# Values of the differential attention by two token tiles with 512 columns instead of two heads with 256, and the second of their products ahead of diff_in(2)

## The chip, the cores and the metric

The kernel runs on one core of a Trainium2 chip, as one launch. The metric is device time in microseconds: the median of 3 runs of the kernel before is 1768.67 us (1768.25 to 1769.67). One execution was profiled; its span is 1766.6 us.

## The reference

A trunk of two layers works on 512 tokens of 1024 features. Each layer norms its input, projects it with one matrix w_in, and mixes it in three branches: differential attention with four heads, a convolution module, and a neighbourhood attention ("natten"). Sigmoid gates merge them, then follow a SwiGLU FFN and a gated input embedding. What matters here, cut:

```python
q, k = apply_rope(q, cos, sin), apply_rope(k, cos, sin)   # per head 2 x 64 columns
v = va.reshape(B, S, HA, DV_A).transpose(0, 2, 1, 3)      # 4 heads x 128 columns
s = jnp.einsum('bhcqd,bhckd->bhcqk', qi, k) * scale
a = jax.nn.softmax(s, axis=-1)
a = a[:, :, 0] - lam * a[:, :, 1]
o = jnp.einsum('bhqk,bhkd->bhqd', a, v)
```

`va` is the normed input (512 x 1024) times 512 columns of w_in.

## The kernel before, in words

All products run as three fp32r matmuls: every operand is split into a high part (ACT copies it, L147) and a low part (DVE subtracts, L161), and high x high, high x low and low x high are added in PSUM. `split` does both. `weights()` brings one weight tile of up to 128 x 1024 (512 KB): a DMA into `wr` on SP's queue, the high part `wh` by ACT, the low part `wl` by DVE. Each of the three has 3 buffers, so a transfer waits until the low part of the tile three earlier is done. These three steps get a priority 400 ahead of their place; the order of ACT, DVE, POOL and of the queues follows from priorities, a scheduler decides it when the program is built. The order of PE is the order in which the code is written. PSUM has 3 buffers `mm`, 2 `sc` (scores), 2 `tr` (transposes) and 1 `av`.

A layer calls in turn glu, natten_in and natten_v, then `diff_in(0)`, `diff_v(0)`, `diff_in(1)`, `gate_c(0)`, `diff_in(2)`, `diff_v(1)`, `diff_in(3)`, the other gates, and after them the branch products, merges, w_o, the FFN and the embedding. `diff_in(head)` projects queries and keys of one head. For both, ACT copies the product to `rp`, four DMAs on SP's queue write the rotated copy (L846), DVE multiplies both with the rope tables and adds them ("rope rows"), splits the sum into `kh` and `rp`, and DMAs stack the parts in `qk` and `x`. Then it queues four attention units with `later(unit, delay, gap)`. Time for these is counted in ticks of four chunks, a chunk being three matmuls of a projection: a unit starts `delay` ticks after it was queued. A unit makes scores (4 matmuls, `diff_sc`), their maximum (TENSOR_REDUCE on DVE), the exponentials on ACT, a reciprocal and a factor with lambda, and `diff_a` on DVE; every second unit then transposes two `diff_a` (`diff_tr`), splits them to `pt`, and multiplies with the values (`diff_av`). The natten units run the same way, their products being `natten_mm` (3 buffers `mm` are shared with the projections), evicted in two DVE rows `natten_y`.

`diff_v(g)` calls `values()`: for a pair of heads g, the 256 columns of the pair for all 512 tokens, the tokens stationary and the weights streaming (L619, L621, L623). Two accumulators hold two token tiles each; 8 k-tiles x 4 token tiles x 3 matmuls make 96 matmuls of 256 columns. The weights of a pair are two tiles of 512 KB. Eight evictions of 128x256 to `v` follow in a layer (ACT and DVE each). The taps of the convolution (`conv_z`, L164, 240 in all) are put behind single operations as background work of DVE: one behind the first rope row of each projection, for instance. `gate_b` takes its buffers from `v`.

Of the kernel before, what the change touches and what calls it, by code (L numbers as in the profile page):

```python
# [20 lines left out]
P = 128  # L21
L = 2
# [4 lines left out]
KD = 8  # L27
# [38 lines left out]
class Net:  # L66
# [365 lines left out]
    def layer(self, i, h, xsrc, xs):  # L432
        self.i, self.h = i, h
        zs, cs = [], []
        self.todo = self.taps(zs, cs)
        self.glu(zs)
        if i == 0:
            self.lambdas()
        yc, ya, yb = [], [], []
        sn, sd = {}, {}  # L440
        self.natten_in(0, sn, yc)
        self.drain(self.renorm)
        self.h = self.hs
        self.natten_v(sn)
        last = self.glu_last(zs)
        self.natten_in(1, sn, yc)
        next(last)
        self.natten_in(2, sn, yc)
        next(last)
        self.natten_in(3, sn, yc)  # L450
        acc, gb = [], []
        self.diff_in(0, sd, ya)
        self.diff_v(0, sd)
        self.diff_in(1, sd, ya)
        self.gate_c(acc, 0)
        self.diff_in(2, sd, ya)
        self.diff_v(1, sd)
        self.diff_in(3, sd, ya)
        for m in range(1, KD):
            self.gate_c(acc, m)  # L460
        for m in range(2):
            self.gate_b(gb, m, AF.Copy, None)
        for g in acc + gb:
            self.act(g, g, AF.Sigmoid, table="sigmoid")
        self.branch_c(acc, yc)
        for m in range(2, 4):
            self.gate_b(gb, m, AF.Sigmoid, "sigmoid")
# [12 lines left out]
        h = self.ffn(h, x)  # L480
        return self.ple(h, x, xs, self.inputs())
# [118 lines left out]

        yield from self.norm(st[0], CB, (3, 1), done)

    def values(self, ap, parts):


        mm = self.nc.tensor.matmul
        accs = [self.ps("mm", (P, 2, 256)) for _ in range(2)]
        for o in range(0, KD, 4):
            wh, wl = self.weights(ap[:, o * 256:(o + 4) * 256], 1024)
            both = [(k, t) for k in range(o, o + 4) for t in range(4)]  # L610
            if o == 0:

                both.sort(key=lambda kt: kt[1] // 2)
            for n, (k, t) in enumerate(both):
                s = slice((k - o) * 256, (k - o + 1) * 256)
                out = accs[t // 2][:, t % 2, :]
                ts = slice(t * P, (t + 1) * P)

                mm(out, self.h[k][:, 0, ts], wh[:, s], start=k == 0 and t % 2 == 0,  # L619
                   stop=False, skip_group_check=True)  # L620
                mm(out, self.h[k][:, 0, ts], wl[:, s], start=False, stop=False,  # L621
                   skip_group_check=True)
                mm(out, self.h[k][:, 1, ts], wh[:, s], start=False,  # L623
                   stop=k == KD - 1 and t % 2 == 1, skip_group_check=True)
                if n % 2:
                    self.chunk()
        vs = []
        for acc in accs:
            v = self.sb("v", [P, 2, 512], F32R)
            for t in range(2):  # L630
                for hi, lo, a in parts(v[:, t], acc[:, t]):
                    self.split(hi, lo, a)
            vs.append(v)
        return vs

# [168 lines left out]
    def gate_b(self, gs, m, func, table):  # L804
        self.phase = "gateb"
        ps = self.proj(OFF_G + D + m * P)
        if m % 2 == 0:
            gs += self.parts_of("v", [512], 2)
        self.background(self.act(gs[m], ps, func, table=table), self.bg["gateb"])

# [19 lines left out]
    def diff_in(self, head, st, ys):  # L830
# [21 lines left out]
            self.stack(nat, low, st4[:, 2 * s:2 * s + 2], k2 if s else None)  # L852
        box = dict(s0=self.sb("sm", [P, 4]))
        for qt in range(4):
            self.later(self.diff_unit(head, qt, st4, k2, st, box, ys), 6 if head else 7, 2)

    def diff_v(self, g, st):
        self.phase = "diff"
        st["v", g] = self.values(self.a["w_va"][self.i, g], lambda v, a: ((v[:, 0:256], v[:, 256:512], a),))

    def diff_unit(self, head, qt, st4, k2, st, box, ys):

# [513 lines left out]
    return np.ascontiguousarray(w).reshape(*lead, m // P, P, (k // P) * P)  # L1376


def _vblocks(w):
    w = w.reshape(L, KD, P, 2, 256).transpose(0, 3, 2, 1, 4)  # L1380
    return np.ascontiguousarray(w).reshape(L, 2, P, KD * 256)
# [52 lines left out]
def _layout(v):  # L1434
# [4 lines left out]
    for i in range(L):  # L1439
# [17 lines left out]
        "w_va": _vblocks(w_in[:, :, OFF_VA:OFF_VA + 512]),  # L1457
# [26 lines left out]
```

## Time and profile before

| what | number |
|---|---|
| median of 3 runs | 1768.67 us (1768.25 to 1769.67) |
| span of the profiled execution | 1766.6 us |
| PE busy, share of the span | 1759.3 us, 100% |
| DVE busy | 1408.6 us, 80% |
| ACT busy | 885.5 us, 50% |
| chain that ended last | PE 92%, DVE 4%, DMA 2%, ACT 2% |
| matmuls of the values | 384 of 256 columns |

The profile shows one execution. Matmuls are pipelined, so a row's duration on PE overlaps the next row; what a matmul costs is read from the start of one to the start of the next. Rows of DVE and ACT overlap by some 0.1 us in the same way. A row of the timeline has its start, its duration, engine, line, operation and tiles, and in brackets the idle time before it and what ended that.

### The profile page before, as it was taken

How to read it: one execution, taken by the hardware profiler on the slowest of the kernel's cores; microseconds unless marked ns; L12 is line 12 of the kernel's file. 1: busy time of each engine (PE TensorE's matmuls, PEld its weight loads, DVE VectorE, ACT ScalarE, POOL GpSimd, SP SyncE). 2: the span in 40 equal slices, each digit the busy share in tenths (PEclk: the TensorE clock that was granted, in tenths of full speed). 3: DMA queues.
4: the chain of work that ended last, by engine and by line, in shares of the span. 5: the costliest groups of instructions: out<-in, count | busy, mean ns of one | idle time of the engine just before them, and what ended most of it. 6: DMA issues, size and time to landing. Idle time of an engine off the chain costs nothing.

```text
span 1766.6 us, 27127 instructions
## 1 busy us (share of the span) xinstructions
PE 1759.3 (100%) x10146; PEld 1551.8 (88%) x10146; DVE 1408.6 (80%) x2354; ACT 885.5 (50%) x1529; POOL 98.4 (6%) x114
## 2 busy tenths in 40 slices
PE   9999999999999999999999999999999999999998
PEld 7888888888899899998888888888888998989987
DVE  7967988998898587787777688889887976867776
ACT  5576555325565254454545655552356643534444
POOL 0000000000111010100000000000001110101000
PEclk9999999999999999999999999999999999999999
DMA  6575641334757365544446655322356674655332
GB/s 231 158 186 160 162 123 54 102 100 150 222 153 196 106 173 156 137 126 127 151 137 173 180 148 154 108 73 94 101 183 194 168 179 118 172 141 156 99 104 96
DMA packets 112548, 253.95 MB, mean 144 GB/s; under 512 B 14368, under 2 KB 23328, under 8 KB 112416
## 3 DMA queue, kind: packets, MB, share of 16 engines
q1 hardware_dynamic: 99024, 227.83, 42.0%
q0 software_dynamic: 12672, 23.07, 8.1%
q8 instruction: 80, 1.31, 0.3%
q10 hardware_dynamic: 720, 1.31, 0.2%
q14 instruction: 52, 0.43, 0.1%
HBM read 214.41 MB, written 7.34 MB: 126 GB/s over the span
## 4 chain that ended last, share of the span: by engine, by line
PE 92%; DVE 4%; DMA 2%; ACT 2%; issue 1%; SPq 0%; POOL 0%; ACTq 0%; POOLq 0%; DVEq 0%
PE ffn_mm L1034 4%; PE ffn_mm L1036 4%; PE ffn_mm L182 4%; PE ffn_mm L181 4%; PE ffn_mm L183 4%; PE ffn_mm L1035 4%; PE ffn_sc L1036 3%; PE ffn_sc L1034 3%; PE ffn_sc L1035 3%; PE mergea_mm L182 2%; PE mergea_mm L183 2%; PE mergea_mm L181 2%; PE gateb_mm L182 2%; PE gateb_mm L183 2%; PE gateb_mm L181 2%; PE wo_mm L182 2%
## 5 line engine op out<-in xcount | busy, mean ns | idle before, releaser
L164 DVE SCALAR_TENSOR_TENSOR conv_z<-glu_z,pre_par,conv_z 128x512 f32<-128x512 f32 x240 | 179.6, 748 | 3.5
L147 ACT ACTIVATE ffn_wh<-ffn_wr 128x1024 fp32r<-128x1024 f32 (+1 forms) x92 | 92.8, 1015 | 111.9 <-PE ffn_mm L182 81.4
L1004 POOL DMA_DIRECT2D ffn_qk<-w_fu x88 | 78.1, 978 | 605.6 <-DMA ffn_qk<-w_fu 289.7
L161 DVE TENSOR_TENSOR ffn_wl<-ffn_wr,ffn_wh 128x1024 fp32r<-128x1024 f32 (+1 forms) x92 | 107.4, 1173 | 5.3 <-ACT ffn_wh L147 4.6
L161 DVE TENSOR_TENSOR ffn_t<-ffn_mm,wo_rb 128x512 f32<-128x512 f32 (+1 forms) x64 | 38.7, 605 | 68.4 <-PE ffn_mm L183 68.4
L147 ACT ACTIVATE mergea_wh<-mergea_wr 128x1024 fp32r<-128x1024 f32 (+1 forms) x32 | 27.1, 848 | 96.8 <-PE mergea_mm L182 79.5
L147 ACT ACTIVATE ffn_wh<-ffn_qk 128x1024 fp32r<-128x1024 f32 x44 | 46.7, 1061 | 37.1 <-PE ffn_mm L182 15.9
L161 DVE TENSOR_TENSOR ffn_wl<-ffn_qk,ffn_wh 128x1024 fp32r<-128x1024 f32 x44 | 53.9, 1224 | 10.7 <-ACT ffn_wh L147 10.7
L161 DVE TENSOR_TENSOR ffn_t<-ffn_t,ffn_t 128x512 f32<-128x512 f32 (+1 forms) x46 | 31.3, 680 | 31.9 <-ACT ffn_t L147 31.4
L147 ACT ACTIVATE natten_e<-natten_e,natten_s 128x192 f32<-128x192 f32 (+1 forms) x88 | 39.3, 474 | 25.2 <-DVE natten_s L726 21.9
L181 PE MATMUL ffn_mm<-ffn_v,ffn_wh 128*128 128x512 f32 x132 | 51.4, 389 | 0.0
L182 PE MATMUL ffn_mm<-ffn_v,ffn_wh 128*128 128x512 f32 x132 | 51.4, 389 | 0.0
L183 PE MATMUL ffn_mm<-ffn_v,ffn_wl 128*128 128x512 f32 x132 | 51.3, 389 | 0.0
L181 PE MATMUL ffn_mm<-ffn_y,ffn_wh 128*128 128x512 f32 x132 | 51.3, 389 | 0.0
L182 PE MATMUL ffn_mm<-ffn_y,ffn_wh 128*128 128x512 f32 x132 | 51.3, 389 | 0.0
L183 PE MATMUL ffn_mm<-ffn_y,ffn_wl 128*128 128x512 f32 x132 | 51.3, 389 | 0.0
L147 ACT ACTIVATE diff_a<-diff_sc,diff_s 128x512 f32<-128x512 f32 x32 | 22.0, 687 | 57.1 <-DVE diff_s L919 57.0
L1036 PE MATMUL ffn_mm<-wo_h,ffn_wl 128*128 128x256 f32 x176 | 49.8, 283 | 0.0
L1036 PE MATMUL ffn_sc<-wo_h,ffn_wl 128*128 128x256 f32 x176 | 49.8, 283 | 0.0
L1035 PE MATMUL ffn_sc<-wo_h,ffn_wh 128*128 128x256 f32 x176 | 49.8, 283 | 0.0
L1035 PE MATMUL ffn_mm<-wo_h,ffn_wh 128*128 128x256 f32 x176 | 49.8, 283 | 0.0
L1034 PE MATMUL ffn_sc<-wo_h,ffn_wh 128*128 128x256 f32 x176 | 49.8, 283 | 0.0
(879 smaller groups left out, 6539.8 us busy)
## 6 DMA issues: line engine op xcount, KB each, us to landing
ffn_qk<-w_fu POOLq DMA_DIRECT2D x88, 256.0 KB, 5.7
ffn_wr<-w_fg SPq DMA_DIRECT2D x44, 512.0 KB, 3.7
ffn_wr<-w_fd SPq DMA_DIRECT2D x32, 448.0 KB, 4.1
ffn_r<-w_fu SPq DMA_DIRECT2D x44, 256.0 KB, 4.2
ffn_qk<-w_fg SPq DMA_DIRECT2D x44, 256.0 KB, 4.0
ffn_qk<-w_fu SPq DMA_DIRECT2D x44, 256.0 KB, 4.2
natten_wr<-w_in SPq DMA_DIRECT2D x16, 512.0 KB, 4.3
diff_wr<-w_in SPq DMA_DIRECT2D x16, 512.0 KB, 4.2
```

What stands on the lines that cost most here:

```text
L147: i = self.nc.scalar.activation(out, in_, func, **kw)
L161: return self.nc.vector.tensor_tensor(out, a, b, op)
L164: return self.nc.vector.scalar_tensor_tensor(out, a, s, b, op0, op1)
L181: mm(out, wh, ah, start=first, stop=False)
L182: mm(out, wh, al, start=False, stop=False)
L183: mm(out, wl, ah, start=False, stop=last)
L1004: nc.gpsimd.dma_start(q, wu[:, lo], accum_op=ALU.add)
L1034: mm(out, wh[:, c], bh, start=first and k == 0, stop=False, skip_group_check=True)
L1035: mm(out, wh[:, c], bl, start=False, stop=False, skip_group_check=True)
L1036: mm(out, wl[:, c], bh, start=False, stop=k == 3, skip_group_check=True)
```

## The change

`values(ap, half)` now makes one half of the tokens (two tiles of 128) for all 512 columns: two accumulators of 128 x 512, one for each token tile, 8 k-tiles x 2 token tiles x 3 matmuls, 48 matmuls of 512 columns. `diff_v(0)` makes tokens 0 to 255, `diff_v(1)` tokens 256 to 511, each with the whole of w_va, whose layout on the host becomes k-tile by k-tile with 512 columns; each call loads it as four tiles of 512 KB. Every unit now needs both halves, so `diff_v(1)` moves ahead of `diff_in(2)`, and the first head's units start 9 ticks after they are queued instead of 7. A half is evicted in two splits of 128x512. Two of the gates' buffers come from `kh`, since `v` is held in another shape.

```diff
         self.gate_c(acc, 0)
+        self.diff_v(1, sd)
         self.diff_in(2, sd, ya)
-        self.diff_v(1, sd)
...
-    def values(self, ap, parts):
+    def values(self, ap, half):
...
-        accs = [self.ps("mm", (P, 2, 256)) for _ in range(2)]
-        for o in range(0, KD, 4):
-            wh, wl = self.weights(ap[:, o * 256:(o + 4) * 256], 1024)
-            both = [(k, t) for k in range(o, o + 4) for t in range(4)]
...
-                mm(out, self.h[k][:, 0, ts], wh[:, s], start=k == 0 and t % 2 == 0,
-                   stop=False, skip_group_check=True)
...
+        accs = [self.ps("mm") for _ in range(2)]
+        for o in range(0, KD, 2):
+            wh, wl = self.weights(ap[:, o * 512:(o + 2) * 512], 1024)
+            for k in (o, o + 1):
+                s = slice((k - o) * 512, (k - o + 1) * 512)
+                for t, out in enumerate(accs):
+                    hi, lo = (a[:, (2 * half + t) * P:(2 * half + t + 1) * P] for a in self.halves(self.h[k]))
+                    mm(out, hi, wh[:, s], start=k == 0, stop=False)
+                    mm(out, hi, wl[:, s], start=False, stop=False)
+                    mm(out, lo, wh[:, s], start=False, stop=k == KD - 1)
                     self.chunk()
...
-            for t in range(2):
-                for hi, lo, a in parts(v[:, t], acc[:, t]):
-                    self.split(hi, lo, a)
+            self.split(v[:, 0], v[:, 1], acc)
...
-        if m % 2 == 0:
+        if m == 0:
+            gs += [self.sb("kh", [P, 512]) for _ in range(2)]
+        elif m % 2 == 0:
             gs += self.parts_of("v", [512], 2)
...
-            self.later(self.diff_unit(head, qt, st4, k2, st, box, ys), 6 if head else 7, 2)
+            self.later(self.diff_unit(head, qt, st4, k2, st, box, ys), 6 if head else 9, 2)
...
-        cs = slice((head % 2) * P, (head % 2) * P + P)
+        cs = slice(head * P, head * P + P)
...
-                v = st["v", head // 2][kp][:, u].rearrange("p (a b) -> p a b", a=2)
+                v = st["v", kp][u]
```

On PE the second product of values stands behind the gate. In layer 0, these are PE's rows at the end of `gate_c(0)` before (L181 to L183 are the projections' matmuls, `diff_mm` an accumulator in an `mm` buffer):

```order
849 L181 MATMUL gatec_mm_1861<-glu_h_558,gatec_wh_1863 128x512
850 L182 MATMUL gatec_mm_1861<-glu_h_558,gatec_wh_1863 128x512
851 L183 MATMUL gatec_mm_1861<-glu_h_558,gatec_wl_1864 128x512
852 L181 MATMUL diff_mm_1926<-glu_h_386,diff_wh_1928 128x512
853 L182 MATMUL diff_mm_1926<-glu_h_386,diff_wh_1928 128x512
854 L183 MATMUL diff_mm_1926<-glu_h_386,diff_wl_1929 128x512
```

And at the same place of the changed kernel:

```order
797 L181 MATMUL gatec_mm_1805<-glu_h_558,gatec_wh_1807 128x512
798 L182 MATMUL gatec_mm_1805<-glu_h_558,gatec_wh_1807 128x512
799 L183 MATMUL gatec_mm_1805<-glu_h_558,gatec_wl_1808 128x512
800 L614 MATMUL diff_mm_1868<-diff_wh_1871,glu_h_386 128x512
801 L615 MATMUL diff_mm_1868<-diff_wl_1872,glu_h_386 128x512
802 L616 MATMUL diff_mm_1868<-diff_wh_1871,glu_h_386 128x512
803 L614 MATMUL diff_mm_1869<-diff_wh_1871,glu_h_386 128x512
```

Where the queries of head 2 followed, the values now follow, and they take two `mm` buffers at once (1868 and 1869), four rows after the gate's last.

DVE's rows in the same stretch of layer 0, from the rope rows of head 1's queries (`diff_rp`) on, before (`diff_wl` are low parts of weights, `diff_v` an eviction of values, `diff_s` with `diff_sc` a maximum of scores):

```order
262 L161 TENSOR_TENSOR diff_rp_1742<-diff_rp_1742,diff_r_1315 128x512
263 L164 SCALAR_TENSOR_TENSOR conv_z_370<-glu_z_321,pre_par_67,conv_z_370 128x512
264 L161 TENSOR_TENSOR diff_wl_2010<-diff_wr_2008,diff_wh_2009 128x1024
265 L161 TENSOR_TENSOR diff_rp_1743<-diff_rp_1743,diff_r_1317 128x512
266 L924 RECIPROCAL diff_s_1810<-diff_s_1810 128x1
267 L161 TENSOR_TENSOR diff_rp_1742<-diff_rp_1742,diff_rp_1743 128x512
268 L161 TENSOR_TENSOR diff_v_1685<-diff_mm_1503,diff_v_1685 128x256
```

And of the changed kernel, from the same rope row to the first low part of weights behind the natten eviction:

```order
261 L161 TENSOR_TENSOR diff_rp_1702<-diff_rp_1702,diff_r_1315 128x512
262 L161 TENSOR_TENSOR diff_wl_1906<-diff_wr_1904,diff_wh_1905 128x1024
263 L164 SCALAR_TENSOR_TENSOR conv_z_370<-glu_z_321,pre_par_67,conv_z_370 128x512
264 L161 TENSOR_TENSOR diff_rp_1703<-diff_rp_1703,diff_r_1317 128x512
265 L161 TENSOR_TENSOR diff_rp_1702<-diff_rp_1702,diff_rp_1703 128x512
266 L161 TENSOR_TENSOR diff_v_1647<-diff_mm_1503,diff_v_1647 128x512
267 L161 TENSOR_TENSOR natten_y_1314<-natten_mm_1824,natten_y_1314 64x512
268 L161 TENSOR_TENSOR diff_rp_1702<-diff_rp_1702,diff_kh_1713 128x512
269 L161 TENSOR_TENSOR natten_y_1314<-natten_y_1314,natten_mm_1824 64x512
270 L910 TENSOR_REDUCE diff_s_1836<-diff_sc_1837 128x1
271 L910 TENSOR_REDUCE diff_s_1836<-diff_sc_1843 128x1
272 L161 TENSOR_TENSOR diff_wl_1924<-diff_wr_1922,diff_wh_1923 128x1024
```

The two `natten_y` rows stand earlier in the changed order, the reciprocal and the maximum rows of head 0 later, and the low parts are of `w_va` (further ones, 1958 and 2001, 2079, stand in rows 277, 282 and 287; the second `diff_a` is row 289).

On SP's queue, the weight transfers between the key transfers of head 0 and the rotated copies of head 1 (L846), before:

```order
97 L175 DMA diff_wr_2008<-w_in 128x1024
98 L664 DMA diff_qk_1319<-diff_kh_1490 64x512 x2
99 L664 DMA diff_x_1320<-diff_kh_1490 64x512 x2
100 L664 DMA diff_qk_1319<-diff_rp_1479 64x512 x2
101 L664 DMA diff_x_1320<-diff_rp_1479 64x512 x2
102 L175 DMA diff_wr_2093<-w_va 128x1024
103 L846 DMA diff_rp_1743<-diff_rp_1742 32x512
104 L175 DMA diff_wr_2179<-w_va 128x1024
105 L846 DMA diff_rp_1743<-diff_rp_1742 32x512 x3
```

And in the changed kernel (the copies are at L837 there):

```order
99 L175 DMA diff_wr_1870<-w_va 128x1024
100 L653 DMA diff_qk_1319<-diff_rp_1399 64x512
101 L653 DMA diff_qk_1319<-diff_kh_1490 64x512 x2
102 L175 DMA diff_wr_1904<-w_va 128x1024
103 L653 DMA diff_x_1320<-diff_kh_1490 64x512
104 L175 DMA diff_wr_1922<-w_va 128x1024
105 L653 DMA diff_x_1320<-diff_kh_1490 64x512
106 L653 DMA diff_qk_1319<-diff_rp_1479 64x512 x2
107 L653 DMA diff_x_1320<-diff_rp_1479 64x512 x2
108 L837 DMA diff_rp_1703<-diff_rp_1702 32x512
109 L175 DMA diff_wr_1956<-w_va 128x1024
110 L837 DMA diff_rp_1703<-diff_rp_1702 32x512 x3
```

The two tiles 1904 and 1922 now stand among the key transfers, where 2093 stood behind them; behind the first copy one weight tile stands in both.

More of the change, by code (lines that the diff above doesn't have):

```diff
@@ L601, in conv @@
         yield from self.norm(st[0], CB, (3, 1), done)
-    def values(self, ap, parts):
+    def values(self, ap, half):
         mm = self.nc.tensor.matmul
-        accs = [self.ps("mm", (P, 2, 256)) for _ in range(2)]
-        for o in range(0, KD, 4):
-            wh, wl = self.weights(ap[:, o * 256:(o + 4) * 256], 1024)
-            both = [(k, t) for k in range(o, o + 4) for t in range(4)]
[L611 to L619, printed above, removed]
-                   stop=False, skip_group_check=True)
[L621 to L625, printed above, removed]
+        accs = [self.ps("mm") for _ in range(2)]
[8 more added lines that the diff above has]
+                    mm(out, lo, wh[:, s], start=False, stop=k == KD - 1)
                     self.chunk()
@@ L854, in diff_in @@
         for qt in range(4):
-            self.later(self.diff_unit(head, qt, st4, k2, st, box, ys), 6 if head else 7, 2)
+            self.later(self.diff_unit(head, qt, st4, k2, st, box, ys), 6 if head else 9, 2)
     def diff_v(self, g, st):
         self.phase = "diff"
-        st["v", g] = self.values(self.a["w_va"][self.i, g], lambda v, a: ((v[:, 0:256], v[:, 256:512], a),))
+        st["v", g] = self.values(self.a["w_va"][self.i], g)
     def diff_unit(self, head, qt, st4, k2, st, box, ys):
@@ L1376, in _blocks @@
     return np.ascontiguousarray(w).reshape(*lead, m // P, P, (k // P) * P)
-def _vblocks(w):
-    w = w.reshape(L, KD, P, 2, 256).transpose(0, 3, 2, 1, 4)
-    return np.ascontiguousarray(w).reshape(L, 2, P, KD * 256)
 def _wide(w):
@@ L1456, in _layout @@
         "w_in": _blocks(w_in),
-        "w_va": _vblocks(w_in[:, :, OFF_VA:OFF_VA + 512]),
+        "w_va": _wide(w_in[:, :, OFF_VA:OFF_VA + 512]),
         "w_vc": _wide(w_in[:, :, OFF_VC:OFF_VC + 512]),
```

## Prediction

> **What bounds the kernel now.** I read the page first, from its top: the busy times, the granted clock and the chain that ended last.
>
> ```profile
> span 1766.6 us, 27127 instructions
> PE 1759.3 (100%) x10146; PEld 1551.8 (88%) x10146; DVE 1408.6 (80%) x2354; ACT 885.5 (50%) x1529; POOL 98.4 (6%) x114
> PEclk9999999999999999999999999999999999999999
> PE 92%; DVE 4%; DMA 2%; ACT 2%; issue 1%; SPq 0%; POOL 0%; ACTq 0%; POOLq 0%; DVEq 0%
> ```
>
> TensorE is the bound: busy for the whole span, at its full granted clock in all 40 slices, and 92% of the chain. So the time is the sum of the distances from the start of one matmul to the start of the next, plus the few places where PE waits. VectorE holds only 4% of the chain, but it is the second engine, and its 80% is a mean. The table by stage says more about the stretch in which the change works:
>
> ```profile
> 170.00:180.00 10.00, 8.92 (x17) 1.00 0.48 138
> 180.00:190.00 10.00, 9.84 (x18) 1.00 0.40 109
> 1056.00:1066.00 10.00, 9.87 (x18) 1.00 0.41 105
> ```
>
> The columns are the stretch, its length, busy time of DVE, granted clock, DMA share and GB/s. In layer 0 VectorE has 0.16 us to spare between 180 and 190, in layer 1 0.13 us between 1056 and 1066. Both are in or next to the place to which the second product of values is moved. There anything that VectorE gets on top must show up as time.
>
> **The change part by part.** *The matmuls.* Before, a stretch of 48 matmuls of 256 columns begins at the first row below and ends where the next group starts; the other two rows give the distance of 512-column matmuls.
>
> ```profile
> L619 PE MATMUL diff_mm<-diff_wh,glu_h x64: 277/283/364, 142.6 to 208.3; 128*128 128x256 f32 x64
> 150.28 0.30 PE L619 MATMUL diff_mm<-diff_wh,glu_h 128*128 128x256 f32 x1
> 156.06 0.25 PE L722 MATMUL natten_sc<-natten_qk 128*128 128x192 f32 x1
> ...
> 139.55 0.39 PE L181 MATMUL diff_mm<-glu_h,diff_wh 128*128 128x512 f32 x1
> 140.23 0.39 PE L181 MATMUL diff_mm<-glu_h,diff_wh 128*128 128x512 f32 x1
> ```
>
> 48 matmuls take 156.06 - 150.28 = 5.78 us, 0.1204 each; three of 512 columns take 140.23 - 139.55 = 0.68, 0.2267 each, and 24 of them 5.44. (The duration column, 283 ns, holds the modelled end of a pipelined matmul and is not the cost.) A stretch thus saves 0.34 us. L619 has 64 rows in layer 0, three lines like it make 192, both layers 384: eight stretches, **-2.7 us**. That is all the change can gain on PE's own work. [...]
>
> *The weights.* Both halves need all of w_va, so it is loaded and split twice: 8 tiles of 512 KB in each layer for 4, which adds 4 transfers on SP's queue, 4 high parts on ACT, 4 low parts on DVE. ACT's 50% hides its four of 1.05 us. The low parts are no free work, by the DVE rows around the place (layer 0):
>
> ```profile
> 167.05 1.23 DVE L161 TENSOR_TENSOR diff_wl<-diff_wr,diff_wh 128x1024 fp32r<-128x1024 f32 x1 [0.53 <-ACT diff_wh L147]
> ...
> 173.27 0.69 DVE L161 TENSOR_TENSOR diff_rp<-diff_rp,diff_r 128x512 f32<-128x512 f32 x1 [0.99 <-DMA diff_rp<-diff_rp]
> 173.88 0.75 DVE L164 SCALAR_TENSOR_TENSOR conv_z<-glu_z,pre_par,conv_z 128x512 f32<-128x512 f32 x1
> 174.54 1.22 DVE L161 TENSOR_TENSOR diff_wl<-diff_wr,diff_wh 128x1024 fp32r<-128x1024 f32 x1
> 175.68 0.69 DVE L161 TENSOR_TENSOR diff_rp<-diff_rp,diff_r 128x512 f32<-128x512 f32 x1
> ...
> 177.01 0.42 DVE L161 TENSOR_TENSOR diff_v<-diff_mm,diff_v 128x256 fp32r<-128x256 f32 x1
> 177.34 0.21 DVE L164 SCALAR_TENSOR_TENSOR diff_s<-diff_s,glu_nlam,diff_sm 128x1 f32<-128x1 f32 x1
> ...
> 179.78 0.69 DVE L161 TENSOR_TENSOR natten_y<-natten_mm,natten_y 64x512 fp32r<-64x512 f32 x1
> 180.51 0.69 DVE L919 TENSOR_REDUCE diff_s<-diff_sc 128x1 f32<-128x512 f32 x1
> ...
> 183.09 0.16 DVE L924 RECIPROCAL diff_s<-diff_s 128x1 f32<-128x1 f32 x1
> ...
> 183.53 0.75 DVE L164 SCALAR_TENSOR_TENSOR diff_a<-diff_e,diff_s,diff_a 128x512 f32<-128x512 f32 x1
> 184.20 1.28 DVE L919 TENSOR_REDUCE diff_s<-diff_sc 128x1 f32<-128x512 f32 x2
> 185.40 0.68 DVE L161 TENSOR_TENSOR diff_rp<-diff_rp,diff_r 128x512 f32<-128x512 f32 x1
> ```
>
> From start to start: a low part of weights 1.14 (174.54 to 175.68), a rope row of 128x512 0.61, a conv tap 0.66, natten_y 0.73, a reduce 0.60 (two from 184.20 to 185.40), reciprocal and lambda row 0.44 (183.09 to 183.53), diff_a 0.67, an eviction of v with 256 columns 0.33. One of 512 columns stands nowhere in the trace; I take 0.61, like the rope row, whose two operands have the same shape; its ends are 0.33 (as 256 columns) and 0.66 (twice that). Four low parts (4.56) less the eviction (8 x 0.33 to 4 x 0.61, -0.2) add 4.4 us of DVE work to each layer.
>
> *The order.* By the order rows above, the second stretch of values now follows gate_c(0) directly. PE reaches it early. Before, the gate's last matmul ends where diff_in(2) begins:
>
> ```profile
> 174.18 0.39 PE L183 MATMUL gatec_mm<-glu_h,gatec_wl 128*128 128x512 f32 x1
> 174.66 0.98 PE L763 MATMUL natten_mm<-natten_pt,natten_v 128*128 128x256 f32 x6
> ...
> 179.36 0.39 PE L181 MATMUL diff_mm<-glu_h,diff_wh 128*128 128x512 f32 x1
> 185.71 1.03 PE L876 MATMUL diff_tr<-pre_ident,diff_a 128*128 128x128 f32 x8
> 189.35 0.39 PE L828 MATMUL diff_sc<-diff_qk 128*128 128x512 f32 x1
> 190.26 0.39 PE L181 MATMUL diff_mm<-glu_h,diff_wh 128*128 128x512 f32 x1
> ```
>
> From 179.36 I take off two stretches (0.68), the first score group of head 0, which its longer delay moves behind (0.91, 189.35 to 190.26), and the 0.25 by which natten_mm was late (174.18 to 174.66 is 0.48, one matmul 0.23; it waited for ACT's copy of the raw key projection, which now runs before it). PE would start the second stretch at 177.5. 48 matmuls (10.88) and two score groups (1.82) later, at 190.2, it wants the transposes of diff_a.
>
> VectorE's side starts from the rope row at 173.27, which waited 0.99 us for the rotated copies on SP's queue:
>
> ```profile
> 168.30 0.39 SPq L175 DMA_DIRECT2D diff_wr<-w_va  x1
> 168.74 6.40 SPq L846 DMA_DIRECT2D diff_rp<-diff_rp  x4
> ```
>
> The copies stand behind the weight transfer at 168.30, which needs the buffer that the low part of 167.05 frees at 168.28. In the changed order one such tile, also of w_va, stands there too. PE's 0.7 us lead would draw all this forward, the two low parts more between 140 and 168 push it back; I leave it at 173.27. From there DVE has, by its order up to the second diff_a, 5 low parts (5.70), 8 rope rows (4.88), one v eviction (0.61), 2 natten_y (1.46), 2 taps (1.32), 5 reduces (3.00), 2 pairs of reciprocal and lambda (0.88) and 2 diff_a (1.34): 29 rows, 19.2 us without a gap, until 192.5. Against 190.2 PE waits 2.3 us. Most of it shows earlier: the second accumulator of the stretch needs the PSUM slot of natten_mm, freed by the second natten_y, the ninth row, at 173.27 + 6.3 = 179.6, while PE wants it at 178.2 (three matmuls after 177.5): 1.4 us, and about 0.9 more at the transposes. Before, diff_a was done at 184.20 and its transposes came at 185.71; the stretch had 1.5 us in hand.
>
> Layer 1 the same way:
>
> ```profile
> 1048.63 0.69 DVE L161 TENSOR_TENSOR diff_rp<-diff_rp,diff_r 128x512 f32<-128x512 f32 x1 [1.86 <-DMA diff_rp<-diff_rp]
> 1048.74 0.39 PE L183 MATMUL gatec_mm<-ple_h,gatec_wl 128*128 128x512 f32 x1
> 1049.14 0.97 PE L763 MATMUL natten_mm<-natten_pt,natten_v 128*128 128x256 f32 x6
> 1056.98 0.39 PE L828 MATMUL diff_sc<-diff_x,diff_qk 128*128 128x512 f32 x1
> 1057.76 0.40 PE L828 MATMUL diff_sc<-diff_x,diff_qk 128*128 128x512 f32 x1
> 1060.73 1.03 PE L876 MATMUL diff_tr<-pre_ident,diff_a 128*128 128x128 f32 x8
> ```
>
> Its stalls that go are 0.17 at natten_mm (0.40 for 0.23) and 0.32 at the scores (1056.98 to 1057.76 is 0.78 for two matmuls), 0.5 in all. It lies 1060.73 - 185.71 = 875.0 later, less the 0.25 by which more of its stalls go than in layer 0: PE is ready at 1065.0; DVE is done at 1048.63 + 19.2 = 1067.8. PE waits 2.8.
>
> *What costs nothing.* The other 48 matmuls of each layer come between 143 and 156, where the new low parts have the idle time ahead of 167 and PE needs no VectorE result at once. The kh buffers for two gates and the larger v tiles come free well before their next user. If that cover is gone, the price is at most the two low parts there, 2.3 us in each layer.
>
> *Sum,* against the profiled execution: -2.7 - 0.25 - 0.5 + 2.3 + 2.8 = +1.65, 1768.3 by its span. The median, 1768.67, lies 2.1 above that span, so I add 2.1: **1770.3 us**. About 0.2% (3.5 us) is what a measurement of this kernel can tell from no change.
>
> **The rivals.** *VectorE keeps up.* If the rope row starts 2.3 to 2.8 us sooner, no new wait appears and the gain stays: -2.7 - 0.75, 1765.2. For it speaks the idle time ahead of the rope rows, 0.99 and 1.86 us; against it that they waited for DMAs which the change does not bring forward by more than 0.7 us.
>
> *The queue (slower).* Three w_va tiles now stand on SP's queue ahead of the copies, among the key transfers of head 0, where two weight tiles stood. Each moves 512 KB, on a DMA share that is 0.48 already. If the rotated copies land later, the run of 29 rows starts later, and with no slack in it PE waits for all of that, twice: it decides from about 1 us a layer (1772.3). Half of such a transfer's 4.2 us landing, 2.1 a layer, gives 1774.5.
>
> ```profile
> diff_wr<-w_in SPq DMA_DIRECT2D x16, 512.0 KB, 4.2
> ```
>
> *The matmuls gain nothing.* In the quoted 512 rows the weights are stationary; here the tokens are, and the weights stream. If these cost 0.241 a piece like a pair of 256, -2.7 is gone: 1773.0. Against it: both kinds load 128 columns of weights, and the 256-column rows stream weights already.
>
> **How the numbers follow.** Forecast 0.53, VectorE keeps up 0.17, the queue 0.23, no gain 0.04, the rest for what I have not seen. The forecast's own range is 1768.9 (rope rows 0.7 sooner, twice) to 1771.8 (v eviction and pairs dearer). The range goes from 1765.2, VectorE keeping up, to 1774.5, the queue. Faster by over 0.2% (under 1765.1) needs the second case and something more: 0.06. Slower (over 1772.2): the queue, no gain and the forecast's upper tail, 0.30. Within: 0.64.
>
> **What would show it.** In the changed profile: 192 matmuls of values at 0.227 from start to start; a pause of 1 to 2 us ahead of the fourth matmul of the second stretch, released by DVE natten_y, and one ahead of diff_tr, released by DVE diff_a; DVE without idle time for 19 us after a rope row near 173. I am wrong if the rope row starts before 171, if the pause names a DMA, or if a new wait stands outside these stretches.

## The result and the profile after

The changed kernel takes 1779.72 us (median, 1779.11 to 1780.21), the kernel before 1769.43 beside it: ratio 1.006, 95% interval 1.0048 to 1.0072. It is 10.3 us slower; 1770.3 was forecast, and the range ended at 1774.5. The profiled execution has a span of 1777.3 us against 1766.6, so the 10.7 us can be looked for in its trace.

The first lines of the page after, to be laid beside those of before:

```profile
span 1777.3 us, 26765 instructions
PE 1760.8 (99%) x9954; PEld 1544.1 (87%) x9954; DVE 1413.5 (80%) x2354; ACT 893.4 (50%) x1529; POOL 97.4 (5%) x114
PE 90%; DVE 5%; ACT 1%; DMA 1%; issue 1%; SPq 0%; POOL 0%; ACTq 0%; DVEq 0%; POOLq 0%
```

DVE is busy for 4.9 us longer: its eight further low parts take 9.7 us, the larger evictions 1.2 less than the smaller ones did, and its other rows are a little shorter in this execution. PE's share of the chain fell by two points: PE waits. The stages outside the attention's stretch, from the branch merges to the FFN and the embedding, last the same to 0.01 us in both traces. All the time is between the first diff_in and the last attention unit, and 0.96 us at the very start, where the 512-column matmuls are 0.427 us apart until 4.9 us before and until 7.2 us after, then 0.23 (PE's first glu row starts at 26.77 and 27.73).

PE's rows with idle time ahead of them, in that stretch of the changed kernel, layer 0 and then layer 1 (in brackets the idle time and what ended it; what the pause adds from start to start is about 0.16 more):

```profile
150.43 0.41 PE L752 MATMUL natten_mm<-natten_a,natten_x 128*128 128x128 f32 x2 [0.50 <-ACT diff_wh L147]
180.71 0.47 PE L614 MATMUL diff_mm<-diff_wh,glu_h 128*128 128x512 f32 x1 [0.74 <-DVE natten_y L161]
193.57 0.98 PE L867 MATMUL diff_tr<-pre_ident,diff_a 128*128 128x128 f32 x7 [0.48 <-DVE diff_a L164]
230.95 0.62 PE L231 MATMUL diff_tr<-pre_ident,diff_rc 128*128 128x128 f32 x4 [3.02 <-DVE diff_pt L161]
...
1029.59 0.41 PE L752 MATMUL natten_mm<-natten_a,natten_x 128*128 128x128 f32 x2 [0.50 <-ACT diff_wh L147]
1059.49 0.47 PE L614 MATMUL diff_mm<-diff_wh,ple_h 128*128 128x512 f32 x1 [0.41 <-DVE natten_y L161]
1072.36 0.98 PE L867 MATMUL diff_tr<-pre_ident,diff_a 128*128 128x128 f32 x7 [0.46 <-DVE diff_a L164]
1109.71 1.08 PE L231 MATMUL diff_tr<-pre_ident,diff_rc 128*128 128x128 f32 x4 [3.02 <-DVE diff_pt L161]
```

The second and third row of each layer are the two pauses that the prediction named, at the places and with the releasers that it named. The first and the fourth it did not have. The fourth is the largest by far: the second transposes of the norm that closes head 0 (L231 spreads the row `diff_rc` over all partitions) need one of the two `tr` buffers in PSUM, and that one still holds the transposed probabilities of head 1, until DVE has split them (`diff_pt`). What DVE did meanwhile:

```profile
220.65 0.69 DVE L220 TENSOR_REDUCE diff_sm<-diff_tr 128x4 f32<-128x512 f32 x1 [1.42 <-PE diff_tr L217]
...
222.53 0.69 DVE L161 TENSOR_TENSOR diff_rp<-diff_rp,diff_r 128x512 f32<-128x512 f32 x1
223.14 0.54 DVE L549 TENSOR_SCALAR conv_z<-glu_z,pre_par 128x512 f32<-128x512 f32 x1
223.60 0.68 DVE L161 TENSOR_TENSOR diff_rp<-diff_rp,diff_r 128x512 f32<-128x512 f32 x1
...
224.32 0.69 DVE L161 TENSOR_TENSOR diff_rp<-diff_rp,diff_rp 128x512 f32<-128x512 f32 x1
...
226.39 0.68 DVE L161 TENSOR_TENSOR diff_rp<-diff_rp,diff_kh 128x512 fp32r<-128x512 f32 x1
226.99 0.68 DVE L161 TENSOR_TENSOR diff_rp<-diff_rp,diff_r 128x512 f32<-128x512 f32 x1
...
228.26 0.68 DVE L161 TENSOR_TENSOR diff_rp<-diff_rp,diff_r 128x512 f32<-128x512 f32 x1
228.86 0.74 DVE L164 SCALAR_TENSOR_TENSOR diff_a<-diff_e,diff_s,diff_a 128x512 f32<-128x512 f32 x1
229.52 0.68 DVE L161 TENSOR_TENSOR diff_rp<-diff_rp,diff_rp 128x512 f32<-128x512 f32 x1
230.12 1.28 DVE L161 TENSOR_TENSOR diff_pt<-diff_tr,diff_pt 128x512 fp32r<-128x512 f32 x2
```

DVE was idle for 1.42 us before 220.65 and then worked almost without a gap to 230.12. Seven rope rows (by their sequence, four of head 2's keys and three of head 3's queries), two taps and a weight split stand ahead of diff_pt in its order; ACT's half of the same split had run at 225.12. The kernel before, at the same place, from the norm's reduce to DVE's diff_pt and PE's transposes, has no rope row there and no pause:

```profile
213.86 0.68 DVE L220 TENSOR_REDUCE diff_sm<-diff_tr 128x4 f32<-128x512 f32 x1
...
218.18 1.22 DVE L161 TENSOR_TENSOR gatec_wl<-gatec_wr,gatec_wh 128x1024 fp32r<-128x1024 f32 x1
219.31 1.28 DVE L161 TENSOR_TENSOR diff_pt<-diff_tr,diff_pt 128x512 fp32r<-128x512 f32 x2
...
220.58 0.60 PE L231 MATMUL diff_tr<-pre_ident,diff_rc 128*128 128x128 f32 x4
```

So it looks as if DVE is not too full here, but its order wrong for PE; the experiments test that.

After the pause in layer 1 the clock falls. The columns are the stretch, its length, busy times of PE, its weight loads, DVE, ACT and POOL (with their number of rows), granted clock, DMA share, GB/s; the first two rows are layer 0, the other two layer 1:

```profile
229.05:232.46 3.41, 1.51 (x9) 1.37 (x10) 3.41 (x6) 0.63 (x1) 0.00 (x0) 1.00 0.89 206
232.46:235.87 3.41, 3.41 (x20) 2.92 (x19) 3.02 (x7) 2.87 (x6) 0.00 (x0) 1.00 0.86 264
1106.28:1109.69 3.41, 0.42 (x2) 0.01 (x1) 3.41 (x7) 0.63 (x1) 0.00 (x0) 1.00 0.88 204
1109.69:1113.10 3.41, 3.39 (x10) 2.89 (x11) 3.01 (x5) 1.31 (x3) 0.00 (x0) 0.50 0.84 239
```

The same pause of 3.02 us in layer 0 left the clock at 1.00; the last section has both beside the pauses of other kernels. In layer 1 the 512-column matmuls were some 0.42 us apart for 0.227. The same rows, from the transposes to the third matmul of the gate, took 3.43 us (1109.71 to 1113.14) for 1.85 in layer 0 (230.95 to 232.80), so the clock adds 1.58 us.

The account of the 10.7 us of span, from start to start: the values' matmuls -2.25 (below), the old pauses of before gone -0.75; natten_mm 2 x 0.66; the second stretch 0.90 + 0.64 and 0.57 + 0.62; the norm's transposes 2 x 3.18; the clock 1.58; a pause of 0.32 in each layer between diff_tr and gate_b, and 0.96 at the start. Together 10.6. Without the start, which is not the change's, the two layers make 9.6 of it.

### The profile page after: what moved, and what is told of

Same layout as the page of the kernel before. It is cut to its first block, busy times and chain, and to the rows that moved or that the text cites. A ratio compares the mean times of both kernels' runs of the same rounds, so it can differ in the third digit from the quotient of the medians.

```text
span 1777.3 us, 26765 instructions
## 1 busy us (share of the span) xinstructions
PE 1760.8 (99%) x9954; PEld 1544.1 (87%) x9954; DVE 1413.5 (80%) x2354; ACT 893.4 (50%) x1529; POOL 97.4 (5%) x114
## 4 chain that ended last, share of the span: by engine, by line
PE 90%; DVE 5%; ACT 1%; DMA 1%; issue 1%; SPq 0%; POOL 0%; ACTq 0%; DVEq 0%; POOLq 0%
PE ffn_mm L1025 4%; PE ffn_mm L1027 4%; PE ffn_mm L181 4%; PE ffn_mm L183 4%; PE ffn_mm L182 4%; PE ffn_mm L1026 4%; PE ffn_sc L1027 3%; PE ffn_sc L1025 3%; PE ffn_sc L1026 3%; PE mergea_mm L181 2%; PE mergea_mm L183 2%; PE mergea_mm L182 2%; PE gateb_mm L181 2%; PE wo_mm L181 2%; PE wo_mm L183 2%; PE wo_mm L182 2%
## 5 line engine op out<-in xcount | busy, mean ns | idle before, releaser
L161 DVE TENSOR_TENSOR diff_wl<-diff_wr,diff_wh 128x1024 fp32r<-128x1024 f32 x32 | 39.1, 1221 | 18.0 <-ACT diff_wh L147 12.4
L181 PE MATMUL ffn_mm<-ffn_v,ffn_wh 128*128 128x512 f32 x132 | 51.4, 389 | 0.0
L183 PE MATMUL ffn_mm<-ffn_v,ffn_wl 128*128 128x512 f32 x132 | 51.3, 389 | 0.0
L181 PE MATMUL ffn_mm<-ffn_y,ffn_wh 128*128 128x512 f32 x132 | 51.3, 389 | 0.0
L183 PE MATMUL ffn_mm<-ffn_y,ffn_wl 128*128 128x512 f32 x132 | 51.3, 389 | 0.0
L910 DVE TENSOR_REDUCE diff_s<-diff_sc 128x1 f32<-128x512 f32 x64 | 42.4, 683 | 10.0 <-PE diff_sc L819 10.0
L1026 PE MATMUL ffn_sc<-wo_h,ffn_wh 128*128 128x256 f32 x176 | 49.8, 283 | 0.0
```

The costliest lines, as they stand in the source:

```text
L161: return self.nc.vector.tensor_tensor(out, a, b, op)
L181: mm(out, wh, ah, start=first, stop=False)
L183: mm(out, wl, ah, start=False, stop=last)
L910: nc.vector.tensor_reduce(out=m[:, u:u + 1], in_=sc, op=ALU.max, axis=AX.X, negate=True)
L1026: mm(out, wh[:, c], bl, start=False, stop=False, skip_group_check=True)
```

## The experiments

The large pause has two explanations. ORDER: diff_v(1) used to lie between diff_in(2) and diff_in(3); now the rope rows of both heads come one behind the other, and get ahead of diff_pt. LOAD: four more low parts of weights in each layer make DVE late. The first four kernels are set on this.

### e1: the move alone

```diff
-        self.diff_in(2, sd, ya)
-        self.diff_v(1, sd)
+        self.diff_v(1, sd)
+        self.diff_in(2, sd, ya)
...
-            self.later(..., 6 if head else 7, 2)
+            self.later(..., 6 if head else 9, 2)
```

> The kernel before, with diff_v(1) called ahead of diff_in(2) and head 0's delay 9, and nothing else: 256 columns, each pair's weights split once. Theory ORDER (the change's large wait, 3.18 us ahead of the closing transposes of head 0's norm in each layer, comes from the rope rows of diff_in(3) that VectorE now has in its order ahead of the eviction diff_pt, because diff_v(1) no longer lies between diff_in(2) and diff_in(3)): the wait stays at about 3 us in each layer, 1769.4 + 6.4 = 1775.8, or 1777 if a clock drop follows it. Theory LOAD (the four more low parts of weights in each layer make VectorE late everywhere): no such wait, 1769 to 1770.

1773.87 us, ratio 1.0025 (1.0016 to 1.0035): the move costs 4.5 us without a single 512-column product or extra weight. PE's rows of e1 in layer 0:

```profile
158.06 0.47 PE L181 MATMUL diff_mm<-glu_h,diff_wh 128*128 128x512 f32 x1 [0.95 <-DVE natten_y L161]
228.89 0.62 PE L231 MATMUL diff_tr<-pre_ident,diff_rc 128*128 128x128 f32 x4 [1.44 <-DVE diff_pt L161]
```

The pause at the norm is there without any load, against LOAD, but it is half as long (1.60 and 1.67 from start to start): in e1's order the first diff_pt stands in front of three rows that it stands behind in the changed kernel. ORDER holds, its number was too high.

### e2: the second half's low parts left out

```diff
-            wh, wl = self.weights(ap[:, o * 512:(o + 2) * 512], 1024)
+            wh, wl = self.weights(ap[:, o * 512:(o + 2) * 512], 1024, not half)
```

Without the third argument `weights` makes only the high part and returns it twice.

> The changed kernel without the low parts of the weights in the second half of the values (the high part stands in for them, so the values of tokens 256 to 511 lack one correction): same matmuls, same transfers, four DVE rows of 1.14 us less in each layer. ORDER: the 3.18 us waits stay; only the waits at the start of the second stretch and at its transposes go (0.90 + 0.64 and 0.57 + 0.62): about 1777. LOAD: they go too, 1768 to 1770.

1774.45 us, ratio 1.003 (1.0019 to 1.0041), between the two expectations. The pause at the norm is 1.60 and 1.67, as in e1. And the pauses that ORDER gave up to load stay:

```profile
179.92 0.47 PE L617 MATMUL diff_mm<-diff_wh,glu_h 128*128 128x512 f32 x1 [0.65 <-DVE natten_y L161]
193.11 0.98 PE L870 MATMUL diff_tr<-pre_ident,diff_a 128*128 128x128 f32 x7 [0.78 <-DVE diff_a L164]
228.88 0.62 PE L234 MATMUL diff_tr<-pre_ident,diff_rc 128*128 128x128 f32 x4 [1.44 <-DVE diff_pt L161]
```

So taking the four low parts out does not bring the second stretch back in time. It is no clean test of their work there, since the scheduler chose another order too: a maximum row now stands ahead of the second natten_y, and DVE has gaps of 0.70 and 0.82 us in the run. The large pause lost its other half with them, and e3 shows that this too is a matter of diff_pt's place.

### e3: diff_pt ahead of the rope rows

```diff
-            self.split(pp[:, 0], pp[:, 1], pt)
+            with self.tc.high_priority(offset=min(60, self.tc.cur_priority - self.p0)):
+                self.split(pp[:, 0], pp[:, 1], pt)
```

> The changed kernel with a higher priority (60) for the two splits of the transposed probabilities, diff_pt, so that they stand ahead of the rope rows in VectorE's order; everything else as in the change. ORDER: both 3.18 us waits go, and with them the 1.3 us at a lower clock: 1779.7 - 7.7 = 1772.0. LOAD: VectorE has the same work and only the place of the wait changes: 1778 to 1780.

1773.62 us, ratio 1.0025 (1.0015 to 1.0035): 6.1 us of the 10.3 are gone, with every matmul, transfer and split still there. PE no longer waits at that place of e3:

```profile
227.06 0.39 PE L183 MATMUL gatec_mm<-glu_h,gatec_wl 128*128 128x512 f32 x1
227.28 0.60 PE L231 MATMUL diff_tr<-pre_ident,diff_rc 128*128 128x128 f32 x4
```

This settles the large pause: it is the place of diff_pt in DVE's order. 7.7 was expected; 0.35 us came back at head 1's closing norm (258.73), and 0.38 in each layer behind the first transposes.

### e4: the double load alone

```diff
+            self.weights(ap[:, (4 - o) * 256:(8 - o) * 256], 1024)
             wh, wl = self.weights(ap[:, o * 256:(o + 4) * 256], 1024)
```

This is in the kernel before.

> The kernel before with every w_va tile loaded and split twice (the first copy unused): four more transfers, high parts and low parts in each layer, at the change's places for the first two, no move, 256 columns. ORDER: no large wait; what the change shows at natten_mm (0.66 in each layer) and a part of the VectorE-bound waits, 1770 to 1773. LOAD: most of the loss, 1777 to 1780.

1775.15 us, ratio 1.0031 (1.002 to 1.0042), 5.8 us, between both. No pause at the norm, but others, in layer 0:

```profile
142.43 0.62 PE L764 MATMUL natten_av<-natten_pt,natten_v 128*128 128x256 f32 x3 [0.95 <-DVE natten_pt L161]
143.29 0.44 PE L764 MATMUL natten_av<-natten_a,natten_x 128*128 128x128 f32 x2 [0.24 <-DVE natten_a L161]
159.41 0.47 PE L181 MATMUL diff_mm<-glu_h,diff_wh 128*128 128x512 f32 x1 [0.50 <-DVE natten_y L161]
```

The low parts push the rows of natten's units behind them. That is where the changed kernel has its first pause, at natten_mm: in its DVE rows `diff_wl` (148.02) and a rope row come ahead of `natten_a` (149.86 to 150.28), which PE wants at 149.8. (The row at 150.43 names ACT's diff_wh as what ended the wait; that ended at 150.31, but what the matmul reads is natten_a.) The load is not free, then; it is just not what made the large pause.

### e5: another buffer for the norm's transposes

```diff
-        bc = self.ps("tr", (P, 4, P))
+        bc = self.ps("tr" if eps is None else "sc", (P, 4, P))
```

> The changed kernel with the second transposes of the attention's norm in a PSUM buffer of the scores (sc) instead of the transposes (tr); VectorE's order hardly differs. Theory SLOT (those transposes wait for nothing but one of the two tr buffers, which diff_pt frees late): both 3.18 us waits go, 1779.7 - 6.4 - 1.3 = 1772 to 1774 as with diff_pt moved forward. Rival (they wait for the norm's own chain, or the DVE rows are late for everything): the wait stays, 1778 to 1780.

1787.08 us, ratio 1.0104 (1.0089 to 1.0119): worse than both. The transposes no longer wait, and the next scores do, longer, for the same DVE:

```profile
232.12 0.79 PE L819 MATMUL diff_sc<-diff_qk 128*128 128x512 f32 x1 [3.82 <-DVE diff_t L161]
```

The stretch behind it, with the granted clock in the third column from the end:

```profile
233.00:237.30 4.30, 4.30 (x11) 3.33 (x11) 2.21 (x5) 1.26 (x4) 0.00 (x0) 0.50 0.80 222
```

Neither expectation holds. The scores' buffer is now held until diff_t, which stands behind the rope rows as diff_pt does. A buffer elsewhere is no cure where the row that frees it is late; and the granted clock behind the pause of 3.82 us was 0.50, its mean over the execution 0.996.

### e6: one weight tile for the second half

```diff
-            wh, wl = self.weights(ap[:, o * 512:(o + 2) * 512], 1024)
+            if o == 0 or not half:
+                wh, wl = self.weights(ap[:, o * 512:(o + 2) * 512], 1024)
```

This is on top of e3.

> The changed kernel with diff_pt forward (as in e3) whose second half loads and splits one w_va tile and uses it for all k-tiles, so the values of tokens 256 to 511 are not the reference's: three transfers, high parts and low parts less in each layer. If the second load makes the remaining waits of the second stretch (0.78 + 0.62 + 0.38 in layer 0, 0.83 + 0.65 + 0.38 in layer 1), they go: 1773.6 - 3.6 = 1770.0, and less the natten wait in the first stretch (0.66 each, which stays) the matmuls' 2.7 us are there. If the order makes them: 1773.

1775.55 us, ratio 1.0037 (1.0023 to 1.0052), with less work no faster than e3. The waits at the second stretch's transposes went, that at its second accumulator stayed (0.69 and 0.51 for 0.78 and 0.83), and a new one came at head 1's scores:

```profile
244.09 0.50 PE L820 MATMUL diff_sc<-diff_qk 128*128 128x512 f32 x1 [2.10 <-ACT diff_a L147]
```

Neither theory had this. With three splits less the scheduler's order is another, and in it another row is late for PE.

### e7 and e8: all that waits moved forward, in the changed kernel and in the one before

```diff
-            self.split(pp[:, 0], pp[:, 1], pt)
+            with self.tc.high_priority(offset=min(60, ...)):
+                self.split(pp[:, 0], pp[:, 1], pt)
...
-SOON = 20
+SOON = 60
...
-BG = dict(..., diff=1, gatec=2, ...)
+BG = dict(..., diff=0, gatec=3, ...)
```

The rows from the reciprocal to diff_a and natten's evictions natten_y get the same priority.

> The changed kernel with all that the waits ask for: diff_pt, the reciprocal to diff_a rows, and natten's splits and evictions with priority 60, and the conv taps moved from the projections of this stretch (1 to 0 each) to the gates (2 to 3 each). If the waits are VectorE's order and load in this stretch alone, all of them but about 1 us in each layer go: 1779.7 - 10 = 1768 to 1770. If VectorE is simply too full there: 1772 to 1774.

> The kernel before with the same priorities and taps as e7. Before had next to no waits here (0.36 us in layer 0, 0.6 in layer 1), so 1768.5 to 1769.5. With e7 it shows whether 512 columns pay once the waits are gone: they do if e7 is below this one.

e7: 1772.39 us, ratio 1.0021 (1.0012 to 1.003). e8: 1767.71 us, ratio 0.9993 (0.9984 to 1.0003). What the priorities do for the kernel before cannot be told from nothing, as expected; e7 came out at what "too full" had been given. But its rows say something else. DVE, SP's queue and PE of e7 in layer 0:

```profile
168.02 0.54 SPq L838 DMA_DIRECT2D diff_rp<-diff_rp  x1
168.80 0.39 SPq L175 DMA_DIRECT2D diff_wr<-w_va  x1
169.24 4.28 SPq L838 DMA_DIRECT2D diff_rp<-diff_rp  x4
...
174.32 0.69 DVE L161 TENSOR_TENSOR diff_rp<-diff_rp,diff_r 128x512 f32<-128x512 f32 x1 [2.32 <-DMA diff_rp<-diff_rp]
...
181.18 0.47 PE L614 MATMUL diff_mm<-diff_wh,glu_h 128*128 128x512 f32 x1 [2.00 <-DVE natten_y L161]
```

DVE stood idle for 2.32 us until the rotated copies had landed, and started the run of rows that ends PE's wait 2.3 us late. One copy goes out, then a weight tile of 512 KB, then the other three (the last of the four in that row belongs to the keys). That is the queue that the prediction had as a rival.

### e9 to e11: the copies on ACT's DMA queue

```diff
-                self.nc.sync.dma_start(rot[32 * b:32 * b + 32], raw[32 * o:32 * o + 32])
+                self.nc.scalar.dma_start(rot[32 * b:32 * b + 32], raw[32 * o:32 * o + 32])
```

e9 is on top of e3, e10 of e7, e11 of e8.

> As e3 (the changed kernel with diff_pt forward), and the rotated copies of the rope issued on ACT's DMA queue instead of SP's, where a w_va tile stands among them. Theory QUEUE (the rope rows of head 1 start at 173 to 174 because the copies share SP's queue with a 512 KB tile, and the waits at the second stretch of values follow from that): the rope row starts 1.5 to 2 us sooner and the waits at the second accumulator and the transposes (0.78 + 0.62 and 0.83 + 0.65 in e3) go: 1773.6 - 2.9 = 1770.7. If the copies' own time or VectorE's load makes them: 1773 to 1774.

> As e7 (all priorities, taps at the gates), with the copies on ACT's DMA queue. In e7 the rope row waited 2.3 us for the copies, and the second stretch 2.17 and 1.43 us. QUEUE: these go, 1772.4 - 3.6 = 1768.8. Otherwise 1772 to 1773.

> As e8 (before with the same priorities and taps), with the copies on ACT's DMA queue: the control of e10. It had two waits of 0.3 us left, so 1767 to 1768.5. If 512 columns pay once nothing waits, e10 is below this one by up to 2.7.

1797.12 (ratio 1.0159, 1.0145 to 1.0173), 1777.23 (1.0048, 1.0034 to 1.0061) and 1781.12 us (1.0069, 1.0057 to 1.0082). All expectations failed, the control's too: e11 has two new pauses of 2.71 us at the scores, in the kernel of before. With the copies issued from ACT, its rows come later: DVE waits 2.37 us for ACT's half of natten_y in e11 (until 170.00; 1.12 us, until 167.74, in e8), and 3.22 us in e10 (until 173.00), where e7 starts that row at 168.69 without a wait. That the issuing holds ACT up is my reading of these waits. So these runs say nothing on SP's queue. In e9 the rope row started later (174.72), not sooner.

### e12 and e16: the delay and the place by themselves

> The kernel before with head 0's delay 9 and diff_v(1) in its old place: what of e1's 4.5 us the delay makes, what the place. In this order three rope rows stand ahead of the second diff_pt, in e1 nine ahead of the first. If the place decides: no wait at the norm's transposes, 1769 to 1770. If the delay does: 1772 to 1774.

> The kernel before with diff_v(1) ahead of diff_in(2) and the delay left at 7 (e1 had the place and the delay 9: +4.5 us; e12 the delay alone: +3.1). If place and delay add up, 1769.3 + 1.4 = 1770.7. In this order only the second diff_pt has rope rows ahead of it, so a wait of 1 us at most at the norm's transposes.

The delay of 9 alone: 1772.46 us, ratio 1.0017 (1.0008 to 1.0026), +3.3 with a pause of 0.71 at the norm in each layer, and in layer 0 0.91 at diff_in(1) and 0.84 at head 0's scores. The place alone, with the delay at 7: 1775.89 us, ratio 1.0035 (1.0022 to 1.0047), +6.7, more than both together in e1 (+4.5), with its largest pause elsewhere (1.61 us of idle time ahead of transposes at 255.53, ended by DVE diff_t). They do not add up. Either edit changes which rows of DVE meet which unit.

### e13 to e15: the four copies ahead of the tile, on SP's queue

```diff
+                with self.tc.high_priority(offset=min(500, self.tc.cur_priority - self.p0)):
                     self.nc.sync.dma_start(rot[32 * b:32 * b + 32], raw[32 * o:32 * o + 32])
```

e13 is on top of e3, e14 of e7, e15 of e8.

> As e3 (the changed kernel with diff_pt forward), with a higher priority for the four rotated copies of each rope, on SP's queue as before: all four of head 1's queries now stand ahead of the w_va tile that stood behind the first. QUEUE: the rope row that started at 173.0 in e3, after 2.1 us idle, starts 1 to 2 us sooner, and the waits at the second stretch (0.78 + 0.62 and 0.83 + 0.65) shrink by as much: 1773.6 - 2 = 1771.6. Otherwise 1773 to 1774.

> As e7 (the changed kernel with all priorities and the taps at the gates), with the copies ahead as in e13. e7 still waited 2.17 and 1.43 us at the second accumulator and 1.0 at the scores in each layer. QUEUE: the first two go, 1772.4 - 3.4 = 1769. Otherwise 1772.

> As e8 (before with the same priorities and taps), with the copies ahead: the control of e14. e8 waited for 0.3 us only, so 1767 to 1768. If 512 columns pay without waits, e14 is below this one.

e14: 1767.0 us (1766.55 to 1767.41), ratio 0.9987 (0.9978 to 0.9996), faster than the kernel before by 2.2 us, and the only version here whose interval lies below 1. Its SP queue, rope row and second accumulator in layer 0:

```profile
167.08 2.45 SPq L839 DMA_DIRECT2D diff_rp<-diff_rp  x4
169.64 0.51 SPq L175 DMA_DIRECT2D diff_wr<-w_va  x1
...
171.16 0.69 DVE L161 TENSOR_TENSOR diff_rp<-diff_rp,diff_r 128x512 f32<-128x512 f32 x1 [0.71 <-DMA diff_rp<-diff_rp]
...
178.62 0.39 PE L616 MATMUL diff_mm<-diff_wh,glu_h 128*128 128x512 f32 x1
179.07 0.47 PE L614 MATMUL diff_mm<-diff_wh,glu_h 128*128 128x512 f32 x1
```

The four copies go out before the tile, the rope row starts 3.2 us sooner than in e7, and the pause of 2.17 us at the fourth matmul is 0.22. QUEUE was right for this pause; of the 5.4 us between e7 and e14 the expectation had 3.4.

e13: 1779.47 us, ratio 1.0052 (1.0037 to 1.0068), 5.9 us slower than e3. The copies do what they should (the rope row starts at 170.90 for 173.01, and the pause at the second accumulator is gone), but without e7's priorities the scores are now late:

```profile
184.34 0.50 PE L819 MATMUL diff_sc<-diff_qk 128*128 128x512 f32 x1 [1.93 <-ACT diff_e L147]
```

And the clock falls behind the pause; its mean over the execution is 0.997. The stretch in layer 0, granted clock in the third column from the end:

```profile
185.40:188.40 3.00, 3.00 (x9) 2.32 (x8) 2.93 (x8) 1.27 (x3) 0.00 (x0) 0.51 0.84 226
```
 e15: 1771.79 us, ratio 1.0014 (1.0005 to 1.0023), slower than e8 by 4: a pause of 1.70 us at the scores in each layer, which the same edit brought.

What the 512 columns are worth to PE itself is told by the trace: the 192 matmuls of values take 44.1 us in the changed kernel (pauses of over 0.17 taken out; 22.05 of them in layer 0, where e14 has 22.07), the 384 of before 46.3. Whether they pay in the whole kernel is less clear. e14 is 4.8 us below its control e15, which has pauses of its own, and clear of noise against the kernel before. Against e8, the better kernel with 256 columns, it is 0.7 us by the medians, which were not measured side by side and are no further apart than their runs; that gain is not shown.

## Why the prediction was wrong

*The bound and the gain* held. PE was the bound; the matmuls gained 2.25 us for 2.7 (0.2296 us each for 0.2267: behind natten's rows the first matmul of the values is further from the next, 0.32 us at 143.51 and 0.26 at 151.64). For the same step two matmuls of 256 columns took 241 ns, one of 512 took 230.

*The pauses of before that would go* went, all 0.75 us.

*VectorE's run of 29 rows* was forecast as 19.2 us from the rope row to the end of the second diff_a. The changed kernel has it, from 173.98 to 193.43, 19.45 us. All of this execution lies 0.9 us later from its start (first diff product 128.92 for 128.02); with that taken off, the run goes from 173.1 to 192.5, as forecast. In layer 1, which lies 5.38 later (1008.08 for 1002.70), it starts at 1052.76, 1.25 sooner than taken. The two pauses at the named places cost 1.54 and 1.19 us for 2.3 and 2.8, because PE came later too, having lost 0.66 at natten_mm, and because of the sooner start in layer 1. The added low parts as the reason for them are not confirmed: without four of them the two pauses are there as before (e2), and with the start of the run brought forward they go (e13, e14).

*The step that failed* is the end of that account. I followed DVE's order up to the second diff_a, row 289, and took PE to be free of it from there on; "What costs nothing" named only buffers and the first stretch. Behind row 289 the order before and after differ again: with diff_v(1) gone from between diff_in(2) and diff_in(3), rope rows stand ahead of diff_pt, and two tr buffers are all there are. That was 6.36 us of pauses and 1.58 of clock, 7.9 of the 8.0 us by which the sum was short of what the layers show (9.6 for 1.65); the other errors nearly cancel. The prediction's last sign of being wrong, a new wait outside its stretches, is what came. The order was there to be read: the same walk, continued by 55 rows to the closing norm, would have shown seven rope rows between the norm's reduce and diff_pt, where the kernel before has none.

*"The other 48 matmuls ... PE needs no VectorE result at once"* was wrong as well: natten_mm needs natten_a there, 2 x 0.66. The price that I gave for a lost cover, 2.3 in each layer, was high enough, but it did not enter the sum.

*The rivals.* The queue was put at 0.23, 1774.5, for copies that land later than before. They did not: counted from each layer's first diff product, the rope row that waits for them starts 0.2 and 1.25 us sooner than in the kernel before. What e14 shows is another thing, that their place behind the tile, which the kernel before has too, sets the start of the run. The result lies beyond this rival for the reason above. "VectorE keeps up" did not happen, "the matmuls gain nothing" neither. No rival had the move itself for a cause, though e1 shows that with its longer delay it costs 4.5 us by itself: I had priced its waits only inside the stretch that was moved.

*The clock* was taken as 1.00 throughout. A pause of 3.02 us cost 1.58 us more than itself in layer 1, where 0.50 was granted behind it, and nothing more in layer 0, at 1.00.

What stays open: why e13 and e15 are late at the scores after copies that come sooner, row by row; and which part of e14's step over e7 is the queue and which the order that came with it (3.2 of 5.4 are at the second accumulator).

## What to carry to other kernels

Where the order of one engine is written by hand and the others' is made by a scheduler, moving a block on the first changes who is neighbour to whom on the others for as long as their backlog lasts; walk the order of every engine that frees a buffer until the two orders agree again, not until the block ends. Look for the row that frees a scarce buffer (here 2 of PSUM) and count what stands ahead of it. Added work on the second engine is judged by the same rows: the splits loaded twice cost 5.8 us in one order (e4) and leave no pause of over 0.32 us in the attention's stretch in another (e14).

## What the runs showed of the hardware

The granted clock was 0.50 for some us behind some pauses of PE, and stayed at 1.00 behind others:

| kernel, layer | PE's idle time, until | granted clock there and behind it, mean of each stretch |
|---|---|---|
| e5, 0 | 3.82 us, 232.12 | 0.50 (232.00 to 237.30), 0.96 (237.40 to 239.00) |
| changed, 1 | 3.02 us, 1109.71 | 0.50 (1109.69 to 1113.10), 1.00 (1113.10 to 1116.00) |
| changed, 0 | 3.02 us, 230.95 | 1.00 (229.05 to 235.87) |
| e6, 0 | 2.10 us, 244.09 | 0.77 (244.00 to 245.20), 0.50 (245.20 to 248.00) |
| e7, 0 | 2.00 us, 181.18 | 1.00 (181.10 to 184.00) |
| e13, 0 | 1.93 us, 184.34 | 0.80 (184.20 to 185.40), 0.51 (185.40 to 188.40), 1.00 (188.40 to 190.00) |
| e1, 0 | 1.44 us, 228.89 | 1.00 (228.80 to 232.00) |

The length of the pause does not settle it: of the two pauses of 3.02 us one was followed by 0.50 and one by 1.00, and the clock fell behind 1.93 us in e13 and not behind 2.00 in e7. What else decides is not shown by these runs.

The four rotated copies, 64 KB each, took about 4 us from the first issue to the rope row that waits for all of them when they went out ahead of the tile (167.08 to 171.16 in e14), and 6.3 when a 512 KB tile went out behind the first (168.02 to 174.32 in e7).
